# Layer and feed-forward entries: where the norm's matmuls, the first panels and some casts stand in the queues

## The chip, the core and the metric

The kernel runs on one core of a Trainium2 chip. The metric is the device time of one execution in microseconds (us). Engines work beside each other, each through its own queue in order: PE (TensorE: matmuls and, as PEld, their weight loads), DVE (VectorE), ACT (ScalarE), POOL (GpSimd) and SP (here only the issue of DMAs).

## The reference

Two transformer layers over 512 latent tokens and 256 context tokens of width 1024. Cut to what matters here:

```python
for l in range(DEPTH):                      # two layers
    a_lat = modulate(h_lat, sh_a, sc_a)     # rms_norm(x) * (1 + scale) + shift
    a_ctx = modulate(h_ctx, csh_a, csc_a)
    o_lat, o_ctx = mixer(a_lat, a_ctx)      # layer 0: MLA + neighbourhood heads; layer 1: sliding window
    h_lat = h_lat + g_a * o_lat
    h_lat = h_lat + g_f * swiglu(modulate(h_lat, sh_f, sc_f), w_gate_up[l], w_down[l])
    # the context stream the same way, in layer 0 only
return rms_norm(h_lat, final_norm)
# swiglu: g, u = split(h @ w_gate_up); (silu(g) * u) @ w_down
```

## The kernel before

**Numbers.** Activations lie with features on the 128 partitions, in 8 tiles (`k` = 0 to 7) of 128 features by tokens. Each float32 operand is cut in two parts: ACT *casts* it to the high part (`S.copy`), and DVE or POOL *splits* off the low part (`x - high`). A product is three matmuls: high x high, high x low, low x high. `three` (L747) issues these for one `k`, `mm3` (L311) for a whole sum over `k`. `load_w` (L299) loads a weight panel by a DMA on SP into a `wr` buffer, casts it into `wh` (L305, ACT) and splits it into `wl` (L306, DVE). There are three buffers each of `wr`, `wh` and `wl`, each of 1024 columns.

**Norms.** A `Norm` goes with the projection that writes its input (`output`, L1104): for every tile `m` the residual is added on DVE (L1097), ACT squares it (L347) and DVE or POOL adds the squares up (L350). When a token stream is through, `rest` runs: `rstd` sums the columns by one-column matmuls with `ones` (L364), takes root and reciprocal (L365, L366), makes a diagonal of it on DVE (L367) and spreads it over the partitions by another matmul (L372) into a PSUM bank `pso`. Then `use` modulates tile by tile. The dictionary `marks` keeps the last add and the last diagonal for others to refer to.

**Order.** The code is a program order with priorities; the framework's planner simulates a timeline and lays out every engine's queue from it. `behind(ins, x)` adds a dependency without a semaphore of its own: `ins` is placed after `x` in the plan.

**Feed-forward entry.** The tokens are in two streams, `cs` = far and near: far (second half) is normed first, near last. `combined` gives for each half the high and low parts in the lists `ops`: "12" and "22" for far, "11" and "21" for near. For near, `use` modulates `k` and `k + 4` into one tile (`modulated_to`, L1164 on DVE and L1165 on ACT) and then cuts both at once (`several`, casts L339, splits L340). From the halves `sums` makes further operands T1 to T4. `first_pairs` (L1292) does the first `DIRECT[l]` gate and up panels directly (one pair in layer 0, three pairs in layer 1), a half of the tokens at a time: `half(n, 1)` is panel `n` by far tokens, 8 steps of `three`. The far halves of the first two or three panels run while the near norm is on its way, `bg(2)` follows in layer 0 (two pieces of the modulation vectors of layer 1, `mods_pe`: matmuls L190, copies L192, picks L194), then come the near halves, one panel after the other. The later pairs (`Pair`, L1235) use fewer products, and take casts, splits and sums of weights (L1218, L1219, L1252 to L1260) and T1 to T4. The results of gate panels go through SiLU on ACT (L1307), up panels are multiplied in on DVE (L1309).

**Layer 1 entry.** The last down projection of layer 0 (`final0`) makes the input of layer 1, latent stream first, then context, with `norm1`. Around L1392 three panels are loaded, the two of k and v (`kv`) and that of query pair 0: kv's second split is behind the add mark, the query's split behind the diagonal. Their latent products go side by side into three banks. Query 0 is rotated on POOL (L442 to L444) and cut by `put_q` (cast L699 on ACT, split L700 on POOL); then kv's context products follow, whose banks ACT empties (L834, L726), and the other seven queries.

Of the kernel before, what the change touches and what calls it, by code (L numbers as in the profile page):

```python
# [12 lines left out]
ALU = mybir.AluOpType  # L13
# [12 lines left out]
DIRECT = (1, 3)  # L26
CHUNKS = ((0, 4), (4, 4), (8, 4), (12, 4), (16, 3), (19, 3)), ((0, 3), (3, 3), (6, 4), (10, 4), (14, 4), (18, 4))
# [72 lines left out]
def hybrid_kernel(ctx: ExitStack, tc, I, out):  # L100
# [73 lines left out]
    MOD = {}  # L174
# [3 lines left out]
    def mods_pe(l, comp, get):  # L178

        one = float(comp in (1, 4))  # L180
        for v in range(2):
            MOD[l, comp, v] = T(f"mod{l}{comp}{v}", [P, 8])
        for c in range(4):
            o = get()
            for k in range(KT):
                if k % 2 == 0:
                    w = T("st", [P, 512]) if comp == 1 else T(("ph", "pl")[k // 2 % 2], [P, 512])
                    dma(w, I["mod_wp"][PE_MODS.index((l, comp)), c, k // 2])
                g = slice(32 * (k % 4), 32 * (k % 4) + 32)
                PE.matmul(o[g, :NX], cond_col[:, k], w[:, NX * (k % 2) : NX * (k % 2) + NX], start=k < 4, stop=k > 3)  # L190
            t, d = T("p", [P, NX]), get()
            S.copy(t, o[:, :NX])  # L192
            for m in range(2):
                PE.matmul(d[:, 2 * m : 2 * m + 2], t[:, m * P : (m + 1) * P], pick, start=True, stop=True)  # L194
# [105 lines left out]
    def load_w(src, kt, m, eng=None, tag=None, after=()):  # L300

        r = T("wr", [P, kt * m])
        dma(r, src)
        h, lo = (B(F32R, tag)[:, : kt * m] if tag else T(x, [P, kt * m], F32R) for x in ("wh", "wl"))
        S.copy(h, r)  # L305
        behind((G if eng else V).tensor_tensor(lo, r, f(h), op=ALU.subtract), *after)  # L306
        return tuple(x.rearrange("p (k m) -> p k m", k=kt) for x in (h, lo))
# [27 lines left out]
    def split(src, eng=None, dst=None):  # L335

        p, n = src.shape
        h, lo = dst or (B(F32R), B(F32R))
        S.copy(h[:p, :n], src)  # L339
        (eng or V).tensor_tensor(lo[:p, :n], src, f(h[:p, :n]), op=ALU.subtract)  # L340
        return h, lo

    def square_sum(acc, src, c, tag="p", eng=None):

        n = c.stop - c.start
        t = B(tag=tag)
        S.activation(t[:, :n], src[:, c], AF.Square)  # L347
        if acc is None:
            return t
        marks["add"] = (eng or V).tensor_tensor(acc[:, :n], acc[:, :n], t[:, :n], op=ALU.add)  # L350
        return acc
# [3 lines left out]
    def rstd(acc, nfeat, c, r, get=PQ, tag="p"):  # L355
# [6 lines left out]
        for i in range(m):  # L362
            for j, a in enumerate(accs):
                PE.matmul(d[:, i : i + 1], a[:, i * P : (i + 1) * P], ones[:, :1], start=j == 0, stop=j == len(accs) - 1)  # L364
# [4 lines left out]
        for i in range(0, n, 512):  # L369
            w = min(512, n - i)  # L370
            d = get() if r is not None else PS("o")
            PE.matmul(d[:, :w], ones, diag[:, i : i + w], start=True, stop=True)  # L372
            if r is None:
                return d
            S.copy(r[:, c.start + i : c.start + i + w], d[:, :w])
# [25 lines left out]
    class Norm:  # L401
# [290 lines left out]
    def put_q(ts, scale, hi=None, lo=None):  # L692


        def use(src, c):
            for side, t in enumerate(ts):
                r, x = slice(64 * side, 64 * side + 64), slice(64 - 64 * side, 128 - 64 * side)
                if scale is None:
                    (hi or S.copy)(t[r, c], src[r])  # L699
# [24 lines left out]
    def put(t, rows=P, scale=1.0):  # L724
        def use(src, c):
            S.activation(t[:rows, c], src, AF.Copy, scale=scale)  # L726
# [21 lines left out]
    def three(o, a, b, first, last):  # L748
        PE.matmul(o, a[0], b[0], start=first, stop=False)
        PE.matmul(o, a[0], b[1], start=False, stop=False)  # L750
        PE.matmul(o, a[1], b[0], start=False, stop=last)

# [393 lines left out]

    def combined(src, l, comp, c1, c2):
# [13 lines left out]
        def modulated_to(t, src, k, r, c, at):  # L1161
            for x, v in pieces(c):
                d = t[:, at + x.start - c.start : at + x.stop - c.start]
                V.scalar_tensor_tensor(d, src[:, x], mod(l, comp + 1, v, k), r[:, x], op0=ALU.mult, op1=ALU.mult)  # L1164
                S.activation(d, d, AF.Identity, bias=mod(l, comp, v, k), scale=1.0)  # L1165

        def several(t, names, tag):

            dst, n = (B(F32R, tag), B(F32R, tag)), len(names) * w
            h, lo = split(t[:, :n], dst=dst)  # L1170
            for i, x in enumerate(names):
# [3 lines left out]
        def use(k, r, c, v):  # L1175
# [16 lines left out]
            modulated_to(near[i], src[k], k, r, c, at)  # L1192
# [21 lines left out]

        return Norm(src, use, G if l else None, (0, 4, 1, 5, 2, 6, 3, 7)), ops, sums

    def parts(t, h, lo):
        S.copy(h, t)  # L1218
        V.tensor_tensor(lo, t, f(h), op=ALU.subtract)  # L1219
# [15 lines left out]
    class Pair:  # L1235


        def __init__(self, l, j, ops, cs, tag):
# [3 lines left out]
        def weights(self):  # L1242
# [6 lines left out]
            parts(g, *w1)  # L1249
            self.g1, self.g2 = ([x[:, y] for x in w1] for y in h)  # L1250
            s1, s2 = T("pl", [P, 512]), T("ph", [P, 512])
            V.tensor_tensor(s1, u[:, h[0]], u[:, h[1]], op=ALU.add)  # L1252
# [3 lines left out]
            V.tensor_tensor(s3, g[:, h[0]], u[:, h[0]], op=ALU.subtract)  # L1256
# [35 lines left out]
    def first_pairs(l, ops, cs, tags):  # L1292
# [5 lines left out]
        def half(n, second):  # L1298
            j, i = panels[n]
            if n not in ws:  # L1300
                ws[n] = load_w(I["w_gu"][l, j, i], KT, P)
            (h, lo), (dst, s), c, a = ws[n], tiles[j], cs[second], (("11", "21"), ("12", "22"))[second]
            o = PG()[:, : cs[0].stop]
            for x, k in enumerate((0, 4, 1, 5, 2, 6, 3, 7)):
                three(o, (h[:, k], lo[:, k]), ops[a[k // 4]][k % 4], x == 0, x == 7)
            if i == 0:
                S.activation(s[:, c], o, AF.Silu)  # L1307
            else:
                V.tensor_tensor(s[:, c], s[:, c], o, op=ALU.mult)  # L1309
                parts(s[:, c], *(x[:, c] for x in dst))  # L1310
# [11 lines left out]
    def ffn(l, ops, sums, cs, tags, more, down, final):  # L1322

        for ci, (k0, kc) in enumerate(CHUNKS[l]):
            hs, last = [], None
            for j in range(k0, k0 + kc):
                if j == 0:
                    hs.extend(first_pairs(l, ops, cs, tags))
# [39 lines left out]
    ffn(0, ops, sums, (TOK1, TOK2), ("st", "st", "b", "b"), lambda j: BG[1][j > 10] if j > 2 else 0, down0, final0)  # L1368
# [24 lines left out]
    last_add, diag = norm1.marks[0]  # L1393
    kv = [load_w(I["w_in1"][8 + i], KT, P, after=(last_add,) if i else ()) for i in range(2)]
# [3 lines left out]
    first_w = *kv, load_w(I["w_in1"][0], KT, P, after=(diag,))  # L1398
# [80 lines left out]
    ffn(1, ops, sums, HALVES, ("st",) * 4, lambda j: 0, down1, final1)  # L1479
# [104 lines left out]
```

## Time and profile before

| | |
|---|---|
| median of 3 runs | 1632.85 us (1632.2 to 1634.54) |
| the profiled execution | 1636.45 us |
| its span, first to last instruction | 1634.7 us |
| mean granted clock of TensorE | 0.978 |
| feed-forward entry of layer 0 | about 485 to 530 us |
| entry of layer 1 | about 1000 to 1075 us |
| feed-forward entry of layer 1 | about 1264 to 1307 us |

In a row of the timeline stand the start, the duration, engine, line, operation, written tile <- read tiles with their shape, the count, and in brackets the idle time of the engine before it and what ended that. In a row of waits stand who waited, for whom, the total in us, how often, and the longest. The rows themselves stand in the prediction.

### The profile page before, as it was taken

To read this page: it belongs to the slowest core of one execution; us is meant where nothing else is said; L and a number is where in the kernel's file an instruction comes from. 1 tells how busy PE (TensorE), PEld (TensorE's weight loads), DVE (VectorE), ACT (ScalarE), POOL (GpSimd) and SP (SyncE) were. 2 spreads that over 40 slices of the span, in tenths; PEclk is the share of its full clock that TensorE was granted. 3 is DMA by queue.
4 is the path that set the end of the run, shared out by engine and by line. 5 is a ranking of instruction groups with operands and counts; after the bars stand their busy time and mean duration, and the time that the engine had idled before them with its cause. 6 is when DMAs were issued, how large, how long until landed. Compare 5 with 4: busy or idle time off the path is not lost. (4 is left out here: it accounts for less than half of the span.)

```text
span 1634.7 us, 26536 instructions
## 1 busy us (share of the span) xinstructions
PE 1550.1 (95%) x9906; PEld 1372.7 (84%) x9906; DVE 1213.4 (74%) x2438; ACT 811.2 (50%) x1652; POOL 316.4 (19%) x319
## 2 busy tenths in 40 slices
PE   4799989999998999999999998999999999999997
PEld 3587867786897999999999897777889898998997
DVE  5994878667578679696867685759877587687685
ACT  5453576677355334242423243457856444454453
POOL 1551733230010111102121212384003000000002
PEclk8999999999999999999999999999999999999998
DMA  9445232101652364636455656131005133223232
GB/s 321 164 162 168 63 115 86 31 11 58 226 194 85 129 213 156 221 132 235 166 210 204 231 186 236 46 104 66 1 1 183 49 109 113 95 99 117 85 104 84
DMA packets 77913, 214.92 MB, mean 131 GB/s; under 512 B 10196, under 2 KB 17880, under 8 KB 77784
## 3 DMA queue, kind: packets, MB, share of 16 engines
q1 hardware_dynamic: 60888, 147.16, 27.2%
q0 software_dynamic: 14592, 62.92, 11.0%
q10 hardware_dynamic: 2304, 3.15, 0.5%
q8 instruction: 78, 1.28, 0.3%
q14 instruction: 51, 0.42, 0.1%
HBM read 186.97 MB, written 23.07 MB: 128 GB/s over the span
## 5 line engine op out<-in xcount | busy, mean ns | idle before, releaser
L305 ACT CAST wh<-wr 128x1024 fp32r<-128x1024 f32 (+2 forms) x148 | 113.5, 781 | 223.6 <-PE pss L316 48.5
L306 DVE TENSOR_TENSOR wl<-wr,wh 128x1024 fp32r<-128x1024 f32 (+2 forms) x145 | 135.3, 941 | 89.2 <-ACT wh L305 87.3
L350 POOL TENSOR_TENSOR p<-p,p 128x256 f32<-128x256 f32 (+1 forms) x33 | 32.6, 988 | 477.2 <-ACT p L347 476.2
L539 ACT ACTIVATE p<-p,sm 128x512 f32<-128x512 f32 (+3 forms) x144 | 105.0, 730 | 34.0 <-DVE sm L543 31.8
L214 DVE CUSTOM_DVE_ANT_0 p<-rope,cond 128x1024 bf16<-128x1024 f32 x64 | 77.2, 1222 | 35.6 <-DMA rope<-in_mod_w_dram 35.2
L316 PE MATMUL psd<-b,wh 128*128 128x512 f32 (+3 forms) x266 | 91.2, 343 | 0.2 <-DVE b L1219 0.2
L315 PE MATMUL psd<-b,wh 128*128 128x512 f32 (+3 forms) x226 | 81.6, 361 | 8.5 <-ACT b L1218 5.2
L317 PE MATMUL psd<-b,wl 128*128 128x512 f32 (+3 forms) x226 | 80.1, 354 | 1.6 <-DVE wl L306 1.6
L533 PE MATMUL pso<-ph,b 128*64 128x256 f32 (+1 forms) x384 | 77.6, 361 | 3.1 <-DVE ph L471 3.1
L315 PE MATMUL pss<-st,wh 128*128 128x256 f32 (+2 forms) x233 | 79.3, 340 | 1.4 <-ACT st L1048 0.9
L209 POOL DMA_DIRECT2D rope<-in_mod_w_dram x48 | 25.7, 534 | 283.3 <-DVE mod L214 283.3
L1233 PE MATMUL pss<-b,wl 128*128 128x256 f32 (+1 forms) x258 | 79.3, 308 | 0.7 <-DVE wl L1219 0.7
L1232 PE MATMUL pss<-b,wh 128*128 128x256 f32 (+1 forms) x258 | 79.4, 308 | 0.0
L1231 PE MATMUL pss<-b,wh 128*128 128x256 f32 (+1 forms) x258 | 79.3, 307 | 0.0
L317 PE MATMUL pss<-st,wl 128*128 128x512 f32 (+2 forms) x233 | 79.1, 339 | 0.0
L533 PE MATMUL pso<-pl,b 128*64 128x256 f32 (+1 forms) x384 | 76.9, 359 | 0.2 <-DVE pl L471 0.2
L1231 PE MATMUL pst<-b,wh 128*128 128x384 f32 (+1 forms) x240 | 74.4, 310 | 0.0
L1232 PE MATMUL pst<-b,wh 128*128 128x384 f32 (+1 forms) x240 | 74.3, 310 | 0.0
L1233 PE MATMUL pst<-b,wl 128*128 128x384 f32 (+1 forms) x240 | 73.8, 309 | 0.0
L316 PE MATMUL pss<-b,wh 128*128 128x256 f32 (+3 forms) x228 | 73.3, 324 | 0.4 <-DVE b L1219 0.3
L1231 PE MATMUL psd<-b,wh 128*128 128x384 f32 (+1 forms) x222 | 69.8, 315 | 0.0
L1232 PE MATMUL psd<-b,wh 128*128 128x384 f32 (+1 forms) x222 | 69.8, 314 | 0.0
(548 smaller groups left out, 5516.2 us busy)
## 6 DMA issues: line engine op xcount, KB each, us to landing
wr<-in_w_gu_dram SPq DMA_DIRECT2D x88, 512.0 KB, 4.0
rope<-in_mod_w_dram POOLq DMA_DIRECT2D x48, 512.0 KB, 3.8
wr<-in_w_out_dram SPq DMA_DIRECT2D x32, 512.0 KB, 3.6
wr<-in_w_dn_dram SPq DMA_DIRECT2D x64, 256.0 KB, 3.0
p<-home POOLq DMA_DIRECT2D x40, 384.0 KB, 5.1
home<-p POOLq DMA_DIRECT2D x40, 384.0 KB, 4.5
wr<-in_w_in_dram SPq DMA_DIRECT2D x21, 512.0 KB, 3.5
ph<-in_mod_w_dram SPq DMA_DIRECT2D x24, 256.0 KB, 3.4
```

The costliest lines, as they stand in the source:

```text
L214: V.tensor_tensor_reduce(out=T("p", [P, D], mybir.dt.bfloat16), in0=w, in1=cond[:, v, :], op0=ALU.mult, op1=ALU.add, scale=1.0, scalar=0.0 ...
L305: S.copy(h, r)
L306: behind((G if eng else V).tensor_tensor(lo, r, f(h), op=ALU.subtract), *after)
L315: PE.matmul(o, wh[:, k], mh[:, c], start=first and k == 0, stop=False)
L316: PE.matmul(o, wh[:, k], ml[:, c], start=False, stop=False)
L317: PE.matmul(o, wl[:, k], mh[:, c], start=False, stop=last and k == n - 1)
L350: marks["add"] = (eng or V).tensor_tensor(acc[:, :n], acc[:, :n], t[:, :n], op=ALU.add)
L533: ins = PE.matmul(o[64 * i : 64 * i + 64, c], v(kt), t, start=n == 0, stop=n == len(moving[i]) - 1)
L539: S.activation(p[:, c], p[:, c], AF.Exp, bias=nm, scale=-1.0, accum_out=dn)
L1231: PE.matmul(o, wh, xh, start=first and k == 0, stop=False, skip_group_check=not first)
L1232: PE.matmul(o, wh, xl, start=False, stop=False, skip_group_check=not first)
L1233: PE.matmul(o, wl, xh, start=False, stop=k == 3, skip_group_check=not first)
```

## The change

Six edits:

1. `first_pairs` puts the near norm's matmuls inside the far halves: step 5 (layer 0) or 6 (layer 1) goes behind the last column sum, step 10 or 12 behind the spread. `rest` keeps the marks for it.
2. The near halves of the first two or three panels run side by side: at every `k` one step of each panel. SiLU of these panels goes behind the fourth near cast. `bg(2)` moves behind all direct panels, and the picks of `mods_pe` behind the last step of the near halves.
3. The near modulations from the third pair of tiles on go behind the split of two pairs before.
4. In layer 0 the first `Pair`'s split of g and its first and third sum of weights go behind the fourth near split.
5. In `load_w` the first mark of `after` now holds the cast, the others the split. kv's two panels and query 0's are loaded with the square mark for their casts; in layer 1 the third direct panel is cast behind the last near square and split behind the last near add.
6. `put_q` of query 0 moves behind kv's context products, its casts behind the last evacuation of v (`marks["put"]`).

```diff
+FIRST_STEPS = (5, 10), (6, 12)
...
-                PE.matmul(d[:, 2 * m : 2 * m + 2], t[:, m * P : (m + 1) * P], pick, start=True, stop=True)
+                behind(PE.matmul(d[:, 2 * m : 2 * m + 2], t[:, m * P : (m + 1) * P], pick, start=True, stop=True), *picks)
...
-        S.copy(h, r)
-        behind((G if eng else V).tensor_tensor(lo, r, f(h), op=ALU.subtract), *after)
+        behind(S.copy(h, r), *after[:1])
+        behind((G if eng else V).tensor_tensor(lo, r, f(h), op=ALU.subtract), *after[1:])
...
-            add = marks["add"]
+            self.marks[c.start] = own = dict(marks)
             r = Columns(rstd(acc, D, c, None, PG), c.start)
-            self.marks[c.start] = add, marks["diag"]
+            own.update({x: marks[x] for x in ("sum", "diag", "spread")})
...
-            modulated_to(near[i], src[k], k, r, c, at)
+            modulated_to(near[i], src[k], k, r, c, at, near_done[-2:-1])
...
-        def half(n, second):
-            j, i = panels[n]
-            if n not in ws:
-                ws[n] = load_w(I["w_gu"][l, j, i], KT, P)
+        def half(ns, second):
+            for n in ns:
+                if n not in ws:
+                    ws[n] = load_w(I["w_gu"][l, panels[n][0], panels[n][1]], KT, P,
+                                   after=(own["square"], own["add"]) if n == 2 else ())
...
             for x, k in enumerate((0, 4, 1, 5, 2, 6, 3, 7)):
-                three(o, (h[:, k], lo[:, k]), ops[a[k // 4]][k % 4], x == 0, x == 7)
...
+                for n, o in zip(ns, os):
+                    after = when.pop(len(steps), ())
+                    steps.append(behind(three(o, [y[:, k] for y in ws[n]], ops[a[k // 4]][k % 4], x == 0, x == 7), *after))
...
-        for n in range(min(3, len(panels))):
-            half(n, 1)
-        if l == 0:
-            bg(2)
-        for n in range(len(panels)):
-            if n > 2:
-                half(n, 1)
-            half(n, 0)
+        steps, when = [], {FIRST_STEPS[l][i]: (own[x],) for i, x in enumerate(("sum", "spread"))}
+        ns = range(min(3, len(panels)))
+        for n in ns:
+            half([n], 1)
+        half(ns, 0)
+        picks.append(steps[-1])
+        for n in range(3, len(panels)):
+            half([n], 1)
+            half([n], 0)
...
-                    p = Pair(l, j, ops, cs, tags[j - k0])
+                    p = Pair(l, j, ops, cs, tags[j - k0], (near_done[3],) if j == DIRECT[l] and l == 0 else ())
...
-    last_add, diag = norm1.marks[0]
-    kv = [load_w(I["w_in1"][8 + i], KT, P, after=(last_add,) if i else ()) for i in range(2)]
+    square, last_add, diag = (norm1.marks[0][x] for x in ("square", "add", "diag"))
+    kv = [load_w(I["w_in1"][8 + i], KT, P, after=(square, last_add)) for i in range(2)]
...
-    first_w = *kv, load_w(I["w_in1"][0], KT, P, after=(diag,))
+    first_w = *kv, load_w(I["w_in1"][0], KT, P, after=(square, diag))
...
-    put_q(sets[0], None)(q0[:, LATS], LATS)
...
     drain()
+    put_q(sets[0], None, after=(marks["put"],))(q0[:, LATS], LATS)
```

More of the change, by code (lines that the diff above doesn't have):

```diff
@@ L371, in rstd @@
             d = get() if r is not None else PS("o")
-            PE.matmul(d[:, :w], ones, diag[:, i : i + w], start=True, stop=True)
+            marks["spread"] = PE.matmul(d[:, :w], ones, diag[:, i : i + w], start=True, stop=True)
             if r is None:
@@ L725, in use @@
         def use(src, c):
-            S.activation(t[:rows, c], src, AF.Copy, scale=scale)
+            marks["put"] = S.activation(t[:rows, c], src, AF.Copy, scale=scale)
         return use
@@ L1170, in several @@
             h, lo = split(t[:, :n], dst=dst)
+            near_done.append(marks["split"])
+            near_cast.append(marks["cast"])
             for i, x in enumerate(names):
@@ L1213, in sums, with parts @@
                 several(y, ("T3", "T4"), tag)
+        near_done.clear(), near_cast.clear()
         return Norm(src, use, G if l else None, (0, 4, 1, 5, 2, 6, 3, 7)), ops, sums
-    def parts(t, h, lo):
+    def parts(t, h, lo, after=()):
         S.copy(h, t)
-        V.tensor_tensor(lo, t, f(h), op=ALU.subtract)
+        behind(V.tensor_tensor(lo, t, f(h), op=ALU.subtract), *after)
         return h, lo
@@ L1290, in tail, with first_pairs @@
                 parts(self.s[:, c], *(x[:, c] for x in self.dst))
[L1292 removed]
+    def first_pairs(l, ops, cs, tags, own):
         panels = [(j, i) for j in range(DIRECT[l]) for i in range(2)]
```

57 lines of the change are left out of this document (32 added, 25 removed).

## The prediction

> **What bounds the kernel now.** I read the page first, then the waits of PE alone in the three stretches that the diff touches, then the windows of the stretches in which the granted clock drops.
>
> ```profile
> span 1634.7 us, 26536 instructions
> ...
> PE 1550.1 (95%) x9906; PEld 1372.7 (84%) x9906; DVE 1213.4 (74%) x2438; ACT 811.2 (50%) x1652; POOL 316.4 (19%) x319
> ```
>
> PE is the bound: 1550.1 of 1634.7 us, so 84.6 us are idle, and only these, or slow PE time, can be won by reordering. Waits of PE at the entry of the first feed-forward (485 to 510 us), of layer 1 (1000 to 1070) and of the second feed-forward (1264 to 1290):
>
> ```profile
> PE pst L749 <- ACT b L339: 1.5, 1, 1.5
> PE pst L750 <- DVE b L340: 1.3, 1, 1.3
> PE pss L190 <- issue: 1.1, 1, 1.1
> PE pss L194 <- ACT p L192: 1.0, 1, 1.0
> ```
> ```profile
> PE psd L315 <- ACT b L1218: 5.2, 1, 5.2
> PE pss L749 <- ACT b L398: 1.9, 1, 1.9
> PE psd L315 <- ACT b L834: 1.9, 1, 1.9
> PE psd L317 <- DVE wl L306: 1.6, 2, 1.0
> PE psd L315 <- DVE b L1097: 0.7, 1, 0.7
> ```
> ```profile
> PE pss L749 <- ACT b L339: 2.8, 1, 2.8
> PE pss L750 <- DVE b L340: 0.5, 1, 0.5
> ```
>
> The sums are 4.9, 11.3 and 3.3 us: 19.5 us of the 84.6. Right behind most of these waits the clock is half:
>
> ```profile
> 503.00:509.30 6.30, 4.94 (x20) 4.09 (x21) 6.30 (x12) 3.95 (x7) 0.00 (x0) 0.50 0.56 169
> 1005.30:1010.90 5.60, 5.54 (x13) 4.40 (x14) 2.51 (x4) 0.52 (x2) 0.00 (x0) 0.50 0.34 113
> 1024.30:1028.30 4.00, 4.00 (x22) 4.00 (x22) 3.85 (x8) 2.23 (x5) 2.63 (x4) 0.57 0.18 39
> 1031.00:1034.90 3.90, 3.81 (x10) 2.96 (x11) 3.83 (x6) 3.06 (x7) 1.79 (x2) 0.56 0.25 104
> 1066.40:1072.50 6.10, 6.06 (x14) 4.85 (x15) 6.05 (x7) 4.06 (x6) 3.04 (x2) 0.50 0.70 246
> 1277.10:1284.10 7.00, 6.47 (x29) 6.18 (x30) 3.84 (x8) 3.48 (x9) 0.00 (x0) 0.51 0.01 2
> ```
>
> Columns: stretch, length, PE, PEld, DVE, ACT, POOL busy, clock, DMA share, GB/s. PE busy times (1 - clock) is what the clock costs: 2.5, 2.8, 1.7, 1.7, 3.0 and 3.2 us, 14.9 together. So the entries lose 4.9 + 2.5 = 7.4, then 11.3 + 9.2 = 20.5, then 3.3 + 3.2 = 6.5 us: **34.4 us is the ceiling** of what this change can win where it works.
>
> **The change, part by part.** No instruction, DMA or buffer is added: every `behind` here either ties two instructions of one engine, or (kv splits on DVE behind the add mark, which may be POOL's) only steers the planner without a semaphore. What changes is each queue's order, the order of the halves in `first_pairs`, and the place of `bg(2)`, whose loads on SP, products and picks move with it. What is queued behind a moved instruction is named at each entry.
>
> *First feed-forward.* The rows of PE and DVE, and two windows:
>
> ```profile
> 491.37 0.72 PE L364 MATMUL pst<-ones,p 128*128 128x1 f32 x6
> ...
> 495.67 0.91 PE L372 MATMUL pso<-p,ones 128*128 128x384 f32 x2
> ```
> ```profile
> 487.34 0.55 DVE L350 TENSOR_TENSOR p<-p,p 128x384 f32<-128x384 f32 x1
> ...
> 492.64 0.56 DVE L367 TENSOR_TENSOR p<-ident_r,sm 128x384 f32<-128x384 f32 x1
> ...
> 497.49 4.28 DVE L1164 SCALAR_TENSOR_TENSOR p<-b,mod,pso 128x384 f32<-128x384 f32 x8
> ...
> 504.43 1.82 DVE L340 TENSOR_TENSOR b<-p,b 128x768 fp32r<-128x768 f32 x2
> ```
> ```profile
> 485.09:494.20 9.11, 9.11 (x55) 8.90 (x54) 3.05 (x5) 1.74 (x3) 0.54 (x1) 1.00 0.22 85
> ```
> ```profile
> 500.00:530.00 30.00, 26.63 (x153) 22.97 (x153) 29.72 (x56) 19.06 (x32) 0.00 (x0) 0.89 0.28 88
> ```
>
> The last add of the norm ends at 487.89, yet its column sums stand at 491.37 in PE's queue; the diagonal is done at 493.20, yet the spread stands at 495.67. With 16 steps (calls of `three`) in 9.11 - 0.72 us a step is 0.52 us. Now the sums stand after step 5 (485.1 + 2.6 = 487.7, a wait of 0.2 us) and the spread after step 10 (490.9 with the sums in it). Diagonal to sums is 1.83 us now, so it is ready by 490.0. The spread ends near 491.8 instead of 496.6: 4.8 us earlier, with six steps (3.1 us) of filler behind it. The first DVE split L340 now waits for all eight modulations and more, 497.49 to 504.43; split 0 is now set ahead of modulations 4 and 5, so it can start after four of them (4 x 0.535 = 2.1 us) and one cast. Two panels side by side ask for a new k pair only every 12 products, 2.1 us, and DVE makes one in 2 x 0.535 + 0.91 = 2.0: PE keeps fed, just. That would win all of 7.4 less some 0.5. But DVE is busy 29.72 of 30 us after the entry, and the Pair's split and sums of weights (`near_done[3]`), the SiLU products and `sums()` all queue behind the splits. DVE starts its run 497.49 - 491.8 = 5.7 us earlier, but takes into it the split and the four sums of weights that it did before in idle time (1.2 + 4 x 0.6 = 3.6, the split at the 1.23 of L306 below, the sums estimated at L367's 0.56) and 0.5 of gaps: it ends only 1.6 us earlier. **Between 1.6 and 7.4 I take 3.0**, nearer to the DVE row, since PE has filler there (picks, `bg`, the Pair's first two products). Below zero only if DVE has no slack at all against PE; PE is idle 3.4 of those 30 us, which the waits above explain, so it waits for nothing later there, and I exclude more than 1 us of loss.
>
> *Layer 1.*
>
> ```profile
> 1003.85 1.04 ACT L305 CAST wh<-wr 128x1024 fp32r<-128x1024 f32 x1 [6.88 <-DMA wr<-in_w_in_dram]
> 1004.80 0.51 ACT L1218 CAST b<-p 128x384 fp32r<-128x384 f32 x1
> ...
> 1016.07 1.05 ACT L305 CAST wh<-wr 128x1024 fp32r<-128x1024 f32 x1 [2.69 <-PE pst L316]
> ...
> 1062.00 1.26 ACT L699 CAST st<-b 64x512 fp32r<-64x512 f32 x2 [4.48 <-POOL b L444]
> ```
> ```profile
> 998.11 0.56 DVE L1289 TENSOR_TENSOR p<-p,p 128x384 f32<-128x384 f32 x1
> ...
> 1004.92 1.23 DVE L306 TENSOR_TENSOR wl<-wr,wh 128x1024 fp32r<-128x1024 f32 x1 [6.25 <-ACT wh L305]
> ...
> 1020.56 0.75 DVE L1097 SCALAR_TENSOR_TENSOR b<-psd,mod,b 128x512 f32<-128x512 f32 x1
> ...
> 1029.55 1.39 DVE L397 SCALAR_TENSOR_TENSOR p<-b,mod,pso 128x512 f32<-128x512 f32 x2
> ```
>
> (a) The cast of the last gated product (1004.80) has had its input since 998.67. It stands behind kv's first cast, which waits 6.88 us for a DMA. The change sets that cast behind a square, hence behind it: the wait of 5.2 and the 2.8 of slow clock go. Next late is nothing: the cast could end at 999.2, 6.1 us earlier than its 1005.3, and the wait was 5.2. **8.0**. kv's weight buffer is held longer by that, and nothing here waits for it.
> (b) kv's second cast (1016.07) waits for PE's buffer and holds up squares, adds and the last residual (1020.56): 0.7 us of PE, and with it the norm. **0.7**.
> (c) The norm then starts earlier, and the 1.9 wait plus 1.7 + 1.7 of clock (5.3) could go. Against it, three casts (3 x 1.04) now stand on ACT before or around the square root, and three splits (3 x 1.23) on DVE before the modulations (1029.55), where there were two of each. The mark is read when the norm's generator first runs, after the second context panel, so the casts follow that square. Only the context products, still running on PE, hide them. Bounds: +5.3 to -1.2 (one split more in the chain). **2.0**, below the middle.
> (d) The cast of q0 (1062.00) waited 4.48 us for POOL's rotation while the evacuation L834 and the next weights' cast stood behind it. It goes behind `put`. That frees 1.9 + 1.0 + 3.0 = 5.9; the next weights still need a buffer that kv's context products free at the same place, cast plus split (1.04 + 1.23) less what PE has left, estimated at 0.4: 1.9 us kept. **4.0**, bounds 1 to 5.9. POOL gets q0's lower half later; PE does other queries' products first.
> Layer 1: 8.0 + 0.7 + 2.0 + 4.0 = **14.7**.
>
> *Second feed-forward.*
>
> ```profile
> 1267.56 0.41 DVE L350 TENSOR_TENSOR p<-p,p 128x256 f32<-128x256 f32 x1
> ```
> ```profile
> 1270.43 0.50 PE L364 MATMUL pst<-ones,p 128*128 128x1 f32 x4
> ...
> 1273.75 0.59 PE L372 MATMUL pso<-p,ones 128*128 128x256 f32 x2
> ```
> ```profile
> 1264.68:1274.30 9.62, 9.62 (x80) 9.26 (x78) 3.88 (x8) 3.97 (x8) 1.38 (x1) 1.00 0.47 157
> ```
> ```profile
> 1286.67 1.05 ACT L305 CAST wh<-wr 128x1024 fp32r<-128x1024 f32 x1 [6.10 <-PE pss L750]
> ```
>
> Here 24 steps take 8.6 us, 0.36 each. The last add ends at 1267.97, behind the third panel's split; that split now stands behind the add, which frees 1.1 us, so sums after step 6 (1266.9) wait only 0.2 us. The spread after step 12 ends by 1270.2, 12 steps (4.3 us) ahead of the near products instead of none, more than the old wait of 2.8. So 6.5 goes. New: three panels side by side free their three weight buffers together at the end. Panel 3's cast (1.05; today it starts as soon as one panel is through, 1286.67) and split (1.23) then start about 0.7 us before PE's last product: 1.05 + 1.23 - 0.7 = 1.6 us of new wait, less a step's two first products: 1.5. **6.5 - 0.2 - 1.5 = 4.8**, bounds 1.6 (the new wait halves the clock again, 3.2) and 6.5.
>
> **Sum**: 3.0 + 14.7 + 4.8 = 22.5 us. Against the profiled execution (span 1634.7 us, its own time 1636.45) that is 1613.95; it lay 3.6 above the median of 1632.85, so the forecast is 1632.85 - 22.5 = **1610.4 us**.
>
> **A rule on the clock.** The windows show half clock behind waits of 1.9 us and 2.8 us, and none behind the 0.7. [...]
>
> **The rivals.**
> 1. *DVE becomes the bound, 20%.* For it: 29.72 of 30 us; three splits together at (c). Against it: PE filler. Then 3.0 and 2.0 are lost, and the new wait of 1.5 halves the clock (3.2): 22.5 - 8.2 = 14.3 won, 1618.5 us.
> 2. *The waits go and slow clock stays, 12%*: the clock reacts to the thin column sums (the stretch at 1024.3 stands behind no listed wait of PE but the 0.7 and those sums), not to the gaps. Waits alone: 3.0 x 4.9/7.4 = 2.0; 5.2 + 0.7 + 2.0 x 1.9/5.3 + 4.0 x 2.9/5.9 = 8.6; 3.3 - 1.7 = 1.6. That is 12.2: 1620.7 us. Against it: every other stretch follows a wait.
> 3. *It doesn't do what it says, 11%.* The ties bind a planner that lays out each queue by its own estimate; behind them the orders are drawn anew, and a feed-forward's next weights or POOL's rotations of the queries hand the gain back. Only (a) survives: 1632.85 - 8.0 = 1624.9 us, with a part inside 0.2%.
> 4. *Slower, 7%.* kv's splits are now free only after the add mark, and the modulations are older in the program. If the planner puts the splits behind the latent row of modulations, the three-bank products wait 16 x 0.70 (L397's row) = 11 us for a lower half; behind the context row too, with its norm in between, estimated at twice that and the 2.8 of slow clock behind each wait: 28 us, and 1632.85 - 22.5 + 28 = 1638 us. It decides once that delay is over 22.5 us. Against it: DVE has gaps before the spread, where two splits go today.
>
> **How the numbers follow.** The forecast has the remaining 50%, with 1605 to 1616 as its own range. The range reaches from 1602 (most of the ceiling: 1632.85 - 31) to 1626, over rivals 1, 2 and most of 3. A measurement tells 0.2%, 3.3 us, from no change: faster takes the forecast, rivals 1 and 2 and half of 3, 88%; same, 5%; slower, 7%.
>
> **What would show it.** Right: no PE wait over 1 us between the gated product and the layer-1 squares, clock 1.00 there; kv's casts behind the squares; sums and spread inside the far halves; L699 behind L726. Wrong: the sums still at the end of the far halves, a half-clock stretch behind the near halves of the second feed-forward, PE waiting for `T2`'s operands from DVE in the first, or waits of a microsecond at chunk ends that were not there.

## The result and the profile after

The changed kernel takes 1619.42 us (median of 5 runs, 1617.24 to 1621.04) where the kernel before takes 1633.57 (5 runs beside it on the same chip): ratio 0.9911, 95% interval 0.9896 to 0.9925, 14.2 us less. The profiled spans differ by 1634.7 - 1619.3 = 15.4 us.

The page of the changed kernel, to be laid beside the page of before:

```profile
span 1619.3 us, 26531 instructions
...
PE 1540.7 (95%) x9906; PEld 1365.0 (84%) x9906; DVE 1215.1 (75%) x2438; ACT 812.2 (50%) x1652; POOL 316.9 (20%) x319
```

PE is busy 9.4 us less, which is mostly clock (mean granted 0.984 instead of 0.978), since its 9906 matmuls are the same, and idle for 78.6 instead of 84.6 us. To say where, I call *loss* of a stretch its length minus PE's busy time plus busy time x (1 - granted clock), summed over windows of 10 us. The three entries:

| loss, us | before | changed | won | forecast |
|---|---|---|---|---|
| first feed-forward, 480 to 560 us | 7.0 | 8.3 | -1.3 | 3.0 |
| layer 1, 1000 to 1130 us | 21.3 | 10.0 | 11.3 | 14.7 |
| second feed-forward, 1250 to 1310 us | 6.2 | 1.9 | 4.3 | 4.8 |

Together 14.3 us. A window of 10 us mixes the clock of waiting and of working time; by windows of 1 us the three entries won -1.9, 12.8 and 4.5, together 15.3, next to the 15.4 us between the spans.

**First feed-forward.** The timeline of PE (the sums and the spread), then that of DVE, after:

```profile
489.56 0.83 PE L365 MATMUL pst<-ones,p 128*128 128x1 f32 x6
491.90 0.81 PE L374 MATMUL pso<-p,ones 128*128 128x384 f32 x2
```
```profile
495.82 0.96 DVE L341 TENSOR_TENSOR b<-p,b 128x768 fp32r<-128x768 f32 x1 [0.88 <-ACT b L340]
...
501.60 0.95 DVE L341 TENSOR_TENSOR b<-p,b 128x768 fp32r<-128x768 f32 x1
502.47 1.22 DVE L1227 TENSOR_TENSOR wl<-wr,wh 128x1024 fp32r<-128x1024 f32 x1
503.60 0.68 DVE L1261 TENSOR_TENSOR pl<-wr 128x512 f32<-128x512 f32 x1
...
510.89 0.95 DVE L341 TENSOR_TENSOR st<-p,st 128x768 fp32r<-128x768 f32 x1
...
522.33 0.95 DVE L341 TENSOR_TENSOR st<-p,st 128x768 fp32r<-128x768 f32 x1
```

The rows of DVE in the same stretch before:

```profile
508.45 0.95 DVE L340 TENSOR_TENSOR b<-p,b 128x768 fp32r<-128x768 f32 x1
...
509.79 0.95 DVE L340 TENSOR_TENSOR st<-p,st 128x768 fp32r<-128x768 f32 x1
...
514.74 0.94 DVE L340 TENSOR_TENSOR st<-p,st 128x768 fp32r<-128x768 f32 x1
...
516.08 0.68 DVE L1219 TENSOR_TENSOR wl<-ph,wh 128x512 fp32r<-128x512 f32 x1
```

The near half did what was forecast: the spread ends at 492.7 (forecast 491.8), and the last near split (tile `b`) at 502.55 instead of 509.40. But the first half of the operands T1 to T4 (the four of eight splits that go to tile `st`) ended at 510.74 to 515.68 before and now ends at 511.84 to 523.28; all eight were done by 527.2 and are now by 529.5. Before, DVE went straight from the near splits to them and did the first Pair's weight splits behind them; now the Pair's split and sums, tied behind the near splits, stand in front. PE, 7 us early, runs dry. Its waits between 480 and 545 us, and the windows:

```profile
PE pss L191 <- DMA ph<-in_mod_wp_dram: 3.3, 2, 2.7
PE pss L1239 <- ACT b L340: 0.7, 1, 0.7
PE psd L1240 <- DVE b L341: 0.3, 1, 0.3
```
```profile
500.00:510.00 10.00, 10.00 (x62) 10.00 (x61) 9.97 (x21) 8.74 (x16) 0.00 (x0) 1.00 0.28 87
510.00:520.00 10.00, 6.67 (x35) 1.85 (x33) 10.00 (x17) 2.17 (x3) 0.00 (x0) 0.69 0.57 186
520.00:530.00 10.00, 8.90 (x41) 7.09 (x40) 9.63 (x19) 5.93 (x10) 0.00 (x0) 0.84 0.24 79
```

The longest wait is for a DMA: the second block of modulation products (L191) needs `ph` and `pl`, four buffers each, which the Pair's weights share and of which they held three of `ph` from 505.3 us on. SP issued the next of these loads only 13 us after the last, when PE's own first products of the block (at 510.66) had read that last one:

```profile
497.87 0.43 SPq L134 DMA_DIRECT2D pl<-in_mod_wp_dram  x1
...
511.32 0.33 SPq L134 DMA_DIRECT2D ph<-in_mod_wp_dram  x1
```

That these loads wait for buffers isn't new: before, the Pair's sums held theirs from 496.3 to 516.8. What is new is that PE has nothing else to do: before, the block's products (L190) stood spread between others from 503.08 to 525.0, and now they stand together from 510.66 to 521.1, with the operands for the next products late.

**Layer 1.** ACT, then PE's waits from 1000 to 1030 us:

```profile
1000.50 0.52 ACT L1226 CAST b<-p 128x384 fp32r<-128x384 f32 x1 [1.75 <-DVE p L1298]
...
1013.83 0.81 ACT L348 ACTIVATE p<-b 128x256 f32<-128x256 f32 x2 [1.22 <-DMA parked<-b]
1014.54 2.93 ACT L306 CAST wh<-wr 128x1024 fp32r<-128x1024 f32 x3
1017.49 1.28 ACT L367 ACT_TABLE_LOAD   x1
1018.78 0.26 ACT L367 ACTIVATE sm<-psd,eps 128x4 f32<-128x4 f32 x1
```
```profile
PE pss L751 <- ACT b L400: 2.0, 1, 2.0
PE pso L374 <- DVE p L369: 1.9, 1, 1.9
```

The gated product's cast no longer waits behind kv's weight (5.2 us of PE gone), and the three weight casts stand behind the squares. But all three, 2.93 us, stand in front of the table load and the root. So the norm's chain costs as much as before. By windows:

```profile
1000.00:1010.00 10.00, 10.00 (x51) 8.44 (x50) 6.79 (x11) 4.79 (x8) 3.63 (x3) 1.00 1.03 403
1010.00:1020.00 10.00, 9.10 (x78) 8.90 (x76) 8.10 (x14) 6.74 (x11) 1.92 (x3) 1.00 0.44 158
1020.00:1030.00 10.00, 7.04 (x17) 4.99 (x18) 9.77 (x16) 4.47 (x8) 4.85 (x5) 0.66 0.33 107
...
1060.00:1070.00 10.00, 9.84 (x50) 8.09 (x49) 9.91 (x15) 5.02 (x8) 6.30 (x5) 1.00 0.20 65
...
1090.00:1100.00 10.00, 6.89 (x42) 5.81 (x41) 6.64 (x12) 4.69 (x7) 9.77 (x8) 1.00 0.25 84
```

**Second feed-forward.** PE's waits from 1250 to 1300 us and two windows:

```profile
PE pss L751 <- ACT b L340: 1.0, 1, 1.0
PE psd L751 <- ACT wh L306: 0.5, 1, 0.5
PE pst L751 <- ACT wh L306: 0.3, 1, 0.3
```
```profile
1265.00:1275.00 10.00, 9.22 (x75) 8.81 (x74) 5.45 (x10) 8.01 (x15) 0.00 (x0) 1.00 0.02 3
1275.00:1285.00 10.00, 10.00 (x85) 10.00 (x84) 7.08 (x17) 2.35 (x7) 0.00 (x0) 1.00 0.27 78
```

The half clock is gone. The wait for the panels' weight buffers, freed together, is there, and smaller than the 1.5 us that I gave it. No run undid the edits of this entry one by one.

### The profile page after: what moved, and what is told of

Read it like the earlier page. It is cut to its first block, busy times and chain, and to the rows that moved or that the text cites. A ratio compares the mean times of both kernels' runs of the same rounds, so it can differ in the third digit from the quotient of the medians.

```text
span 1619.3 us, 26531 instructions
## 1 busy us (share of the span) xinstructions
PE 1540.7 (95%) x9906; PEld 1365.0 (84%) x9906; DVE 1215.1 (75%) x2438; ACT 812.2 (50%) x1652; POOL 316.9 (20%) x319
## 3 DMA queue, kind: packets, MB, share of 16 engines
q0 software_dynamic: 14592, 62.92, 11.2%
## 5 line engine op out<-in xcount | busy, mean ns | idle before, releaser
L306 ACT CAST wh<-wr 128x1024 fp32r<-128x1024 f32 (+2 forms) x148 | 113.4, 781 | 204.1 <-PE pss L317 40.6
```

The costliest lines, as they stand in the source:

```text
L306: behind(S.copy(h, r), *after[:1])
```

## The experiments

Each ratio is against the kernel before, run beside it on the same chip. The intervals reach 0.0012 to 0.0016 to each side, about 2 us, so the times separate few of these kernels from the changed one; the losses by stage, from one profile each, tell more. How far such a loss scatters is seen where the code of a stage is the same: the first feed-forward's in four profiles lost 8.3, 8.7, 10.2 and 8.5 us, layer 1's in eight 9.5 to 13.5. "First chunk" is the time from the first far product to the last down product of the first chunk on PE's timeline (changed: 484.80 to 598.67; before: 485.09 to 596.10); it scatters too, from 113.9 to 115.4 in the four profiles with the changed code.

| kernel | ratio, 95% | loss FF 0 | loss layer 1 | loss FF 1 | first chunk |
|---|---|---|---|---|---|
| before | 1 | 7.0 | 21.3 | 6.2 | 111.0 |
| changed | 0.9911 (0.9896 to 0.9925) | 8.3 | 10.0 | 1.9 | 113.9 |
| 1 old entry of FF 0 | 0.9910 (0.9895 to 0.9924) | 7.2 | 12.3 | 1.9 | 110.7 |
| 2 first block early | 0.9931 (0.9919 to 0.9943) | 11.2 | 10.0 | 1.9 | 115.7 |
| 3 Pair untied | 0.9921 (0.9907 to 0.9934) | 6.6 | 13.5 | 1.9 | 111.7 |
| 4 second block late | 0.9908 (0.9893 to 0.9924) | 7.8 | 10.1 | 1.9 | 113.4 |
| 5 splits on POOL | 0.9924 (0.9908 to 0.994) | 11.8 | 9.5 | 1.9 | 116.2 |
| 6 on POOL, untied | 0.9896 (0.9879 to 0.9912) | 7.5 | 10.0 | 1.9 | 112.4 |
| 7 sums and spread only | 0.9907 (0.9894 to 0.992) | 8.2 | 10.2 | 2.5 | 113.4 |
| 8 casts behind diagonal | 0.9928 (0.9916 to 0.9941) | 8.7 | 13.2 | 1.9 | 113.9 |
| 9 one cast early | 0.991 (0.9896 to 0.9923) | 8.5 | 9.2 | 2.0 | 113.9 |
| 10 put_q at its old place | 0.9897 (0.9882 to 0.9912) | 10.2 | 9.8 | 1.9 | 115.4 |
| 11 before + casts alone | 0.9923 (0.9911 to 0.9935) | 7.0 | 8.6 | 6.5 | 111.0 |
| 12 operands first + 9 | 0.99 (0.9887 to 0.9913) | 8.6 | 10.7 | 2.2 | 113.0 |

### What the first feed-forward costs

**1. The old entry.**

```diff
+        if l == 0:
+            for n in range(2):
+                half([n], 1)
+            bg(2)
+            for n in range(2):
+                half([n], 0)
+            return [x for x, _ in tiles]
```

(and the ties of edits 2 to 4 dropped in layer 0).

> The changed kernel with the entry of the first feed-forward as before (far halves, first block of modulation products, near halves one by one, no ties there); layer 1 and the second feed-forward as changed. Theory A (the windows: the entry now loses 8.3 us where it lost 7.0): 1.3 us faster than the changed kernel, about 1618, ratio to before 0.990 to 0.991. Theory B (the prediction: the entry won 3.0 and the windows hide it): 3 us slower, about 1622.5, ratio 0.993. PE idle and slow clock of 485 to 545 us: 7 us in both, at 500 to 510 and not at 510 to 525.

The first chunk is 3.2 us shorter than in the changed kernel, its loss 1.1 us smaller. The total is the same, since layer 1 lost 2.4 us more in this profile, within that stage's scatter. So theory B, a hidden gain of 3.0, is out. By how much the new entry is worse, 1.1 to 3.2 us, one profile doesn't settle; that it is worse, seven do: the three with the old code (before, runs 1 and 11) took 110.7 to 111.0 us for the first chunk, the four with the new code (changed, runs 8, 9 and 10) 113.9 to 115.4.

**2. The first block of modulation products back between far and near halves.**

```diff
+        if l == 0:
+            bg(2)
         half(ns, 0)
...
-                    if l == 0:
-                        bg(2)
```

> The changed kernel with the first block of modulation products back between the far and the near halves of the first feed-forward. Theory A (PE ran dry because the modulation weights of the second block were loaded late): the second block finds other buffers or earlier loads, the waits of L191 for a DMA (3.3 us) go and with them most of the 8.3 us lost at 510 to 525; 3 to 6 us faster than the changed kernel, ratio 0.987 to 0.989. Theory C (DVE makes the operands of T2 too late whatever PE does meanwhile): the waits turn up at the T2 products, behind the splits of DVE; same within 1.5 us, ratio 0.990 to 0.992.

The waits of L191 stayed at 3.3 us, new ones came behind the near splits (L752 behind L341, 1.7 us), and the first chunk is 1.8 us longer than in the changed kernel's profile, but only 0.3 longer than in run 10's, which has the same entry. Neither theory holds, since nothing was won; whether the block is of more use late isn't shown.

**3. The Pair's split and sums without their tie** (edit 4 undone).

> The changed kernel without the tie of the first Pair's split and weight sums behind the last near split. Their buffers (ph, pl) are those of the modulation weights. Theory A (late loads): the buffers come free about 7 us earlier, the waits of L191 for a DMA go, and the entry loses 2 to 5 us less: ratio 0.988 to 0.990. Theory C (DVE is full, and the order on it only moves the loss): the splits of the near halves come later by the split and the sums, 1.2 + 4 x 0.6 us, the near halves wait for them, and the entry loses as much or more: ratio 0.991 to 0.993.

L191 now waits 1.4 us for the DMA and 1.0 for DVE instead of 3.3, and the first chunk is 2.2 us shorter. So the tie costs something; but it goes two ways, and this run doesn't separate them: the loads go out earlier (508.44 instead of 511.32), and the first operand in `st` ends at 505.8 instead of 511.8. What remains is 6.6 us of loss and 111.7 us, no better than before the change, and the time of the whole kernel shows no gain (0.9921).

**4. The second block behind the first Pair's body**, so that PE doesn't stand in front of it in order.

```diff
-                    if l == 0 and j == DIRECT[0]:
-                        bg(2)
                     if last:
                         last.tail()
                     p.body()
+                    if l == 0 and j == DIRECT[0]:
+                        bg(2)
```

> The changed kernel with the second block of modulation products (between head and body of the first Pair) moved behind the Pair's body. Theory A (PE stands in order behind modulation products whose weights are late): the T2 products go ahead of them, the waits of L191 shrink below 1 us, 3 to 5 us faster than the changed kernel, ratio 0.988 to 0.989. Theory C (DVE is the bound): the head ends at 511 us and the T2 operands are split at 511.8, 515.3, 519.8 and 523.3 us as now, so PE waits for these instead, without the filler: as slow or up to 3 us slower, ratio 0.991 to 0.993.

The T2 products went ahead and waited for their operands instead (1.4 + 0.7 + 0.4 us), with 2.7 us left for L191. Loss 7.8: theory C for the larger part.

**5 and 6. Five weight splits of the first Pair on POOL**, with the tie, and without it.

```diff
-            self.s2 = parts(s2, *(x[:, h[0]] for x in w2))
+            self.s2 = parts(s2, *(x[:, h[0]] for x in w2), eng=eng)
...
```

(`eng` is POOL for this Pair alone; `s3`, `s1`, `s4` and `u2` the same way.)

> The changed kernel with five weight splits of the first Pair of the first feed-forward (128x512 each, 0.6 us on DVE) done by POOL, which is idle there (1.3 us each). Theory C (DVE is the bound behind the near halves): 3.0 us less on DVE, the T2 operands and with them the T2 products 2 to 3 us earlier; the entry (first far product to last down product of the first chunk) takes 111 to 112 us instead of 113.9. Theory A (late modulation weights alone): their buffers come free later still, since POOL is slower: 114 to 116 us.

> The same five splits on POOL, and the first Pair's split and weight sums without their tie. If both causes are real (DVE full, and buffers of the modulation weights held by the late sums), the savings add up: the first chunk takes 108 to 110.5 us (111.0 before the change, 113.9 with it, 111.7 without the tie alone), ratio 0.987 to 0.990. If only the buffers count: 111.7 as without the tie alone.

This should have taken 3.0 us from DVE. It didn't: beside POOL's splits, DVE's own instructions took two to three times as long (1.05 to 1.65 us instead of 0.54 to 0.68). POOL and DVE in the run with the tie:

```profile
505.46 1.54 POOL L1227 TENSOR_TENSOR wl<-ph,wh 128x512 fp32r<-128x512 f32 x1 [1.36 <-ACT wh L1226]
...
508.54 1.59 POOL L1227 TENSOR_TENSOR wl<-ph,wh 128x512 fp32r<-128x512 f32 x1
```
```profile
503.21 1.44 DVE L1263 TENSOR_TENSOR ph<-pl,wr 128x512 f32<-128x512 f32 x1
...
505.77 1.65 DVE L1227 TENSOR_TENSOR st<-p,st 128x384 fp32r<-128x384 f32 x1
...
507.94 1.05 DVE L1218 TENSOR_TENSOR p<-b 128x384 f32<-128x384 f32 x1
508.92 1.63 DVE L1219 TENSOR_TENSOR p<-p,p 128x384 f32<-128x384 f32 x1
...
510.60 1.48 DVE L1209 TENSOR_TENSOR p<-b,p 128x384 f32<-128x384 f32 x1
...
513.35 0.54 DVE L1227 TENSOR_TENSOR st<-p,st 128x384 fp32r<-128x384 f32 x1
```

The same instruction, L1227 on 128x384, took 1.65 us beside POOL and 0.54 without it. Against 0.68 us (L1261 above) for the 128x512 and 0.54 for the others, these five lost 0.76 + 1.11 + 0.51 + 1.09 + 0.94 = 4.4 us, more than was taken off. Each of the five ends 0.4 to 0.6 us after the POOL split beside it (507.42 after 507.00, 510.55 after 510.13). Run 6 took 112.4 us for the first chunk, neither the 108 to 110.5 of two savings nor the 111.7 of one; its ratio, 0.9896, is the lowest of all, but its interval covers the changed kernel's 0.9911. So these two runs can't say what less work on DVE would bring.

**7. Only the sums and the spread inside the far halves**; near halves one by one, the block between them, the Pair untied.

> In the first feed-forward only the column sums and the spread inside the far halves, and the near modulations tied to the splits; near halves one by one, the block of modulation products between far and near halves, the first Pair's weights without their tie. Layer 1 and the second feed-forward as changed. Theory C (the loss is made behind the near halves, by DVE's queue and the late modulation weights, and panels side by side only bring PE there sooner with nothing to do): the first chunk takes 108 to 110.5 us (111.0 before, 113.9 as changed). Theory D (panels one by one ask for a pair of operands every 1.04 us, and DVE gives one every 1.93): PE waits 2 to 3.5 us at 497 to 503, slow clock behind it, 111 to 114 us.

Close to theory D: PE waited 1.8 us behind near splits, which come every 1.93 us, 1.8 us for a load and 1.4 for a copy, and the chunk took 113.4. With the Pair untied too, but panels side by side and the block behind them, it took 111.7 (run 3).

### What layer 1's parts are worth

**8 and 9. The three casts behind the diagonal; one behind the last latent square and two behind the diagonal.**

```diff
+            self.last[c.start] = marks["square"]
...
-    kv = [load_w(I["w_in1"][8 + i], KT, P, after=(square, last_add)) for i in range(2)]
+    kv = [load_w(I["w_in1"][8 + i], KT, P, after=(diag if i else norm1.last[0], last_add)) for i in range(2)]
...
-    first_w = *kv, load_w(I["w_in1"][0], KT, P, after=(square, diag))
+    first_w = *kv, load_w(I["w_in1"][0], KT, P, after=(diag, diag))
```

(run 9; run 8 has `(diag, diag)` for all three.)

> The changed kernel with the three weight casts of layer 1 (two of kv, one of q0) tied behind the diagonal of the latent norm, not behind a square. Theory A (term c won nothing because 2.9 us of casts stand in front of the square root on ACT): the root runs at about 1015 instead of 1018.78 us, the spread 3 us earlier, the first three-bank product 2 to 3 us earlier, 2 to 4 us won with the clock behind it; ratio 0.988 to 0.990. Theory B (PE needs all three weights for that product anyway, so casts and splits only move behind the root): the product waits for the splits of q0 instead of the modulations; same within 1 us, ratio 0.990 to 0.992, and worse if modulations queue behind casts.

> The changed kernel with kv's first cast tied behind the last latent square and the other two behind the diagonal. Theory A: the root is delayed by one cast at most (1.0 us) and the splits stand behind it in a chain of two; first three-bank product 2 to 3.5 us earlier than 1024.09 us against the end of the squares, ratio 0.988 to 0.990. Theory B: the product needs q0 last, whose cast and split (1.05 + 1.23 us) follow the second's; as the run with all three behind the diagonal within 1 us.

ACT in run 9:

```profile
1012.75 0.81 ACT L348 ACTIVATE p<-b 128x256 f32<-128x256 f32 x2 [0.28 <-DVE b L1101]
1013.58 1.28 ACT L367 ACT_TABLE_LOAD   x1
1015.37 0.26 ACT L367 ACTIVATE sm<-psd,eps 128x4 f32<-128x4 f32 x1 [0.50 <-PE psd L365]
...
1015.84 1.98 ACT L306 CAST wh<-wr 128x1024 fp32r<-128x1024 f32 x2
```

From the context squares to the root it is 2.62 us instead of 4.95 (1018.78 - 1013.83). In both runs no weight cast stands between these squares and the root. In run 8 PE then waits 2.3 us for the modulations and 2.5 us for a lower half behind them, and nothing is won (0.9928), as theory B says; in run 9 it waits 1.9 and 0.8. Run 9 lost 2.8 us from 1000 to 1050 where the changed kernel lost 6.3, so theory A holds for that stage. But run 9 lost 6.5 instead of 3.7 from 1050 to 1130, where the first scores of the attention wait for DVE (3.2 us). Run 12, with the same casts, lost 4.6 and 6.0. The time stayed. Whether the gain is given back there by necessity is open: other kernels with the layer 1 of the change also show 5.8 and 6.5 in that stretch.

**10. put_q at its old place, without its tie** (edit 6 undone).

> The changed kernel with put_q of query 0 back ahead of kv's context products (and without its tie to the put). Term d of the prediction: 4.0 us, bounds 1 to 5.9. If d is right, ACT stands again behind the cast of q0 waiting for POOL's rotation, PE waits for the evacuation and for the next weights, and 1050 to 1090 us lose 3 to 6 us of PE (idle and slow clock) that the changed kernel doesn't lose (0.2 there): 4 us slower than it, ratio 0.9930 to 0.9945. If the gain of d is given back where the attention starts (the changed kernel loses 3.1 us at 1090 to 1100, waiting for DVE's sums of the softmax): the loss there shrinks by as much, ratio 0.990 to 0.992.

**11. The kernel before with the casts of kv and query 0 tied, and nothing else.**

```diff
-        S.copy(h, r)
-        behind((G if eng else V).tensor_tensor(lo, r, f(h), op=ALU.subtract), *after)
+        behind(S.copy(h, r), *after[:1])
+        behind((G if eng else V).tensor_tensor(lo, r, f(h), op=ALU.subtract), *after[1:])
...
+    kv = [load_w(I["w_in1"][8 + i], KT, P, after=(square, last_add)) for i in range(2)]
...
+    first_w = *kv, load_w(I["w_in1"][0], KT, P, after=(square, diag))
```

> The kernel before with one edit alone: the casts of kv's two weights and q0's tied behind a square (their splits as in the change). The planner then sets the two casts of q0 (64x512) behind the evacuation of the kv panel and ahead of one weight cast by itself. Theory A (the prediction: a and b come from the casts, d from put_q's place and tie): a and b go (8.7 us), the loss at 1060 to 1080 of the kernel before (5.7 us there, and shifted by 8) stays at 3 us or more; ratio 0.9930 to 0.9950. Theory B (d comes with the casts, through the order that the planner draws, as the run with put_q at its old place says): the loss at that place falls below 1.5 us too; 11 to 13 us won, ratio 0.9920 to 0.9935. First and second feed-forward as before: 7.0 and 6.2 us of loss.

Of term (d), nothing is put_q's: run 10 has a ratio of 0.9897, not 0.9930 to 0.9945. With edit 6 undone ACT takes query 0's cast without a wait, in the same place as in the changed kernel:

```profile
1056.63 1.25 ACT L701 CAST st<-b 64x512 fp32r<-64x512 f32 x2
```

and with the casts alone it waits 0.73 instead of 4.48 us, with PE busy all of 1060 to 1080:

```profile
1055.20 1.26 ACT L699 CAST st<-b 64x512 fp32r<-64x512 f32 x2 [0.73 <-POOL b L444]
```
```profile
1060.00:1070.00 10.00, 10.00 (x52) 8.50 (x51) 9.88 (x19) 4.18 (x6) 6.18 (x3) 1.00 0.33 107
1070.00:1080.00 10.00, 10.00 (x50) 8.38 (x49) 5.59 (x16) 7.15 (x12) 9.04 (x8) 1.00 0.30 98
```

With the casts moved, the planner's timeline changed, and it set that cast behind the evacuation by itself. Run 11 wins 0.0077 x 1635 = 12.6 us (10.6 to 14.6): the three edited loads are most of the change. Its second feed-forward, untouched, loses 6.5, which gives that entry's edits 6.5 - 1.9 = 4.6 us. With the 2.9 us that the first chunk lost, the parts come to 12.6 + 4.6 - 2.9 = 14.3 us, where 14.2 were measured.

### A last try at the first feed-forward

**12. Operands first.** The first Pair's sums free, in DVE's idle 3.8 us ahead of the diagonal; its splits and the second Pair's behind the operands; the second block behind the second Pair; in layer 1 the casts of run 9.

> The changed kernel with (1) in the first feed-forward: the first Pair's weight sums free (DVE is idle there for 3.8 us before the diagonal), its other splits and the second Pair's split and sums tied behind the sums of the operands (T1 to T4), the second block of modulation products behind the second Pair's body; and (2) in layer 1: kv's first weight cast behind the last latent square, the other two behind the diagonal. Theory A (DVE's order is what made PE wait: 8.3 us of weight work stands ahead of the first T operand): the operands come by 519.5 instead of 523.3 us, the waits of L191 go, the first chunk takes 107.5 to 110.5 us instead of 113.9; with 3.5 us in layer 1, ratio 0.9855 to 0.9880. Theory B (DVE's amount of work bounds, whatever its order): PE waits behind L341 for the operands instead, 111 to 113.5 us, ratio 0.9885 to 0.9905.

The operands did come as planned, the seventh split by 519.3 us and the eighth by 522.5 (changed: 529.5), and the waits of L191 are gone. PE's longest waits from 480 to 545 us:

```profile
PE psd L1242 <- DVE wl L1228: 2.6, 1, 2.6
PE psd L1240 <- ACT p L1280: 2.6, 1, 2.6
PE psd L1240 <- ACT wh L1227: 0.8, 1, 0.8
```

PE now waits for a weight split that went behind the operands (L1228), and as long for ACT's copy of the head's result (L1280), which stands behind the operands' casts in ACT's queue. Loss 8.6 and first chunk 113.0 are in theory B's range, though PE waits only 0.2 us behind L341, its sign. Of eight new arrangements of this entry (the change and runs 2 to 7 and 12) none took less than 111.7 us; the old one took 110.7 and 111.0. DVE is full from 500 to 520 us in the changed kernel (9.97 and 10.00 of 10), and another order gives PE one product sooner and another later. What less work on DVE would bring stays open, since runs 5 and 6 didn't achieve it. No version was found that is measurably faster than the changed kernel.

## Why the prediction was right or wrong

The forecast was 1610.4 us (1602 to 1626), measured 1619.4: faster, within the range, 9 us short of the forecast and outside the 1605 to 1616 that the forecast kept for itself. Compared with the 22.5 us that were summed, 14.2 came. The number is nearly that of rival 1 (1618.5), and that is luck in part: the 3.0 and the 2.0 were lost, as it says, but the half clock that it adds in the second feed-forward (3.2) didn't come; instead the first feed-forward and (c) fell below zero.

- *First feed-forward, 3.0: wrong in sign,* -1.3 by loss, -2.9 by the first chunk. The step that failed: "PE is idle 3.4 of those 30 us, which the waits above explain, so it waits for nothing later there, and I exclude more than 1 us of loss." DVE's 29.72 of 30 us said the opposite. I moved DVE's start 4.7 us ahead (492.75 instead of 497.49; forecast 5.7), but ordered nothing behind it: the tie of edit 4 that I counted as 3.6 us of work also put that work *in front of* the operands, the first of which came 1.1 us later than before, though the near splits ended 6.9 us earlier. PE had filler "there" only as long as the second block's loads came, and these waited for `ph` and `pl`, which the Pair's sums share. Rival 1 named the row; its sign, PE waiting for T2's operands from DVE, is there, and the larger wait is the DMA's, which no rival named.
- *(a) and (b), 8.7: right.* The wait of 5.2 us, the 2.8 of slow clock behind it and the 0.7 of the last residual are gone, and the 0.9 now at 1010 to 1020 belongs to the norm's chain. Clock 1.00 there, as forecast.
- *(c), 2.0: nothing,* -1.1: the 5.3 us of before are now 1.91 + 1.95 of waits and 2.5 of slow clock (1024.09 to 1029.1 at 0.50), 6.4 together, near the bound of -1.2. The cost was named ("three casts now stand on ACT before or around the square root"), and taken to be hidden by the context products. These ran out at 1019.1, 2 us too soon. Run 9 shows that without two of the casts 3.5 us come at that stage, though not in the time.
- *(d), 4.0: the size came, by another cause.* From 1050 to 1080 the loss fell from 6.25 to 0.16, that is 6.1, and 1.3 were lost again from 1080 to 1120. But put_q's place does nothing (run 10); the moved casts did it through the planner's order (run 11). I priced an edit by the wait that it names, without asking whether another edit removes the same wait.
- *Second feed-forward, 4.8: right,* 4.3. The new wait measured 0.8 (0.5 + 0.3) instead of 1.5, and the one for the near cast 1.0.
- *The clock, rival 2:* wrong as a forecast. Where the waits went, the slow clock went, though the column sums stayed (L365 at 1015.23, 1.62 us; clock 1.00 until 1022). But the stretch at 1024.3 that it was built on does stand behind such sums (L364, 1.72 us; clock 0.57), so what halved the clock there isn't shown (last section), and "none behind the 0.7" contradicts the prediction's own row of that stretch, 0.57.
- *Rival 3,* a redrawn plan: partly so, but in favour of the change.

## What to carry to other kernels

Where an engine has no gap behind an entry (DVE here: 29.72 of 30 us), bringing its work forward decides nothing by itself: write down its queue item by item behind the moved piece, with the buffers that each item holds, and look which consumer comes first. Look first for casts that wait for a transfer at the head of an in-order queue: three moved loads won about 12 of 14 us here. Under a planner, undo each edit alone before crediting it: one of these six did nothing, since another had already redrawn the order.

## What the runs showed of the hardware

**DVE beside POOL's splits.** In run 5, beside POOL's splits of 128x512 (1.54 and 1.59 us in the rows above), four DVE instructions of 128x384 took 1.05 to 1.65 us and one of 128x512 took 1.44, where 0.54 and 0.68 are the times without POOL beside them. Why isn't shown.

**One wait's length didn't tell where the clock halved.** In the changed kernel PE waited 1.91 us, ran the spread and waited 1.95 us; the clock halved inside the second wait and stayed so until about 1029 us. In run 9 the waits at the same place were 1.90 and 0.76, and the clock stayed full. From 1022 us on, changed and run 9:

```profile
1022.00:1029.00 7.00, 5.05 (x13) 3.85 (x13) 6.87 (x11) 4.30 (x8) 3.01 (x3) 0.53 0.31 115
```
```profile
1022.00:1029.00 7.00, 6.57 (x31) 5.48 (x31) 7.00 (x12) 3.45 (x6) 2.22 (x2) 1.00 0.26 89
```

Before, the clock halved behind the single wait of 1.94 us ahead of 1031.09 (0.50 from 1031.6 to 1034.8), and in the first feed-forward it halved at 502.4, inside the third of four waits of which none was over 1.5 us (1.00 from 498.6 to 502.3, 0.50 from 502.5 to 509.2). So a single wait's length doesn't tell these cases apart.

The column sums don't tell them apart either. Before, PE ran the sums of 1.72 us (L364) from 1022.81 us on, behind a wait of 0.7, and the clock was 1.00 from 1021.3 to 1024.6 and 0.50 from 1024.8 to 1028.0; in the changed kernel sums of 1.62 us (L365) ran from 1015.23 us on, and the clock was 1.00 from 1010 to 1022.3. What halves it, no run shows.
